# Score matmuls of the recurrence in blocks of 32 instead of 64 columns, in four visits per head instead of two

## The chip, the cores and the metric

The kernel runs on one core of a Trainium2 chip. A core has a matrix engine (TensorE, PE in the profile, with its weight loads listed as PEld), a vector engine (VectorE, DVE), a scalar engine (ScalarE, ACT), GpSimd (POOL) and SyncE (SP), which issues the transfers. The metric is the device time of one execution in microseconds; the kernel before takes 2050.87 us, the median of three runs (2050.38 to 2050.87).

## The reference, cut to what matters

The network has two layers on 1024 tokens of width 1024. Layer 0 is a sliding-window attention, layer 1 a gated linear recurrence (HGRN2); behind each stands a squared-ReLU MLP. The change is in the recurrence, which runs for 8 heads of width 128 over chunks of 64 tokens:

```python
def chunk_step(state, inp):
    qc, kc, vc, lc = inp                       # lc = log of the forget gate
    b = jnp.cumsum(lc, axis=2)
    o_inter = jnp.einsum('bhtd,bhde->bhte', qc * jnp.exp(b), state)
    diff = b[:, :, :, None, :] - b[:, :, None, :, :]
    decay = jnp.exp(jnp.where(causal[None, None, :, :, None], diff, -jnp.inf))
    scores = jnp.einsum('bhtd,bhtsd,bhsd->bhts', qc, decay, kc)
    o_intra = jnp.einsum('bhts,bhse->bhte', scores, vc)
    b_last = b[:, :, -1]
    new_state = jnp.exp(b_last)[..., None] * state + jnp.einsum(
        'bhsd,bhse->bhde', kc * jnp.exp(b_last[:, :, None, :] - b), vc)
    return new_state, o_inter + o_intra
```

The score of token t for an earlier token s in the same chunk is a sum over the 128 features of q at t, k at s, and the product of the forget gates between them, which differs by feature.

## The kernel before, in words

Tiles are 128 partitions by 512 columns (half of the tokens; NH = 2 halves). Large matmuls are done in Strassen form with each float32 operand split into two parts, wh and wl for weights.

The kernel doesn't issue instructions directly. Every operation is recorded (`op`, `mm`, `tt`, `copy`, ...) with an assumed cost; a planner (`Schedule.forward` and `backward`, lines 197 to 356) simulates the engines with these costs four times, and the order that ends first in its own model is issued. So all instructions carry line 433, the line of the common helper, and groups are told apart by tile names: `t`, `a`, `m`, `wr`, `wh`, `wl` are rotating buffers in SBUF, `p` and `q` banks of PSUM (four each), `d` tensors in HBM, `c` constants. A matmul has the form "whole" or "columns" (it uses some of the array's columns only); the planner adds an assumed drain where the form changes.

`recurrence` (line 1513) handles one head. It keeps q and k transposed (features on partitions, 512 tokens in columns). The decay between two tokens is built by doublings: `double` (line 1647) with H = 1, 2, 4, ..., 64 multiplies, in each pair of neighbouring blocks of H tokens, the later block's q and the earlier block's k by the total decay of the other block (VectorE, 256 columns each, four products per doubling and head), and merges the totals. With `apart`, the result goes into a new tile and the unchanged half is copied there by ScalarE (four copies of 256 columns); without, it is done in place. Before, the doublings by 1, 2, 8, 16 and 32 go apart and those by 4 and 64 are in place.

After the doubling by H, the product of k and q is right for pairs of tokens that lie in neighbouring blocks of H tokens: level lg (H = 1 << lg). So the scores of a chunk are assembled from the diagonal (`own`: q and k themselves), six levels, and `cross`, which takes two chunks of 64 together, because everything behind the scores works on 128 tokens. A matmul of a level has one chunk of 64 keys as stationary operand and the 32 later tokens of the same chunk as moving one. Its 64 output rows are the upper or the lower half of the PSUM partitions, so two groups of columns of the array are used in turn. `merge` writes a level into `scores` with a masked copy on VectorE (`copy_predicated`, 128 partitions by 256 columns).

All these matmuls of a head stand in two bursts, called visits here: the first (lines 1551 to 1565) behind the doubling by 2 with the diagonal and levels 0 to 2, the second (1576 to 1587) behind the doubling by 32 with levels 3 to 5 and the cross. Each matmul lists all operands of its visit as inputs (`late`), so that a visit starts only when all of them are there. Then (1590 to 1597) three copies per half lay the scores into a block of 128 by 128 per pair of chunks, and a memset clears the corner.

`hgrn` (line 1792) runs head e's gates (the input projections, nearly all TensorE) beside head e - 1's recurrence, piece by piece; the last head's recurrence runs beside the first matmuls of the output product (`hgrn_out`, line 1720).

Of the kernel before, what the change touches and what calls it, by code (L numbers as in the profile page):

```python
# [22 lines left out]
TH = T // NH  # L23
# [11 lines left out]
BPH = NBLK // NH  # L35
# [102 lines left out]
HALF = {"ACT": 125.0, "DVE": 105.0}  # L138
# [240 lines left out]
class Net:  # L379
# [1011 lines left out]
    def hgrn_constants(self):  # L1391
        bounds = self.const((P, 2 * KT))
        self.dma(bounds, self.io["lb"], 4 * P * 2 * KT)
        l0, l1 = (bounds[:, i * KT : i * KT + KT] for i in range(2))
        top, e0, e1, lb = (self.const((P, KT)) for _ in range(4))
        self.tt("DVE", top, l0, l1, ALU.max, KT)
        for e, l in ((e0, l0), (e1, l1)):
            self.tt("DVE", e, l, top, ALU.subtract, KT)
            self.act(e, e, AF.Exp, KT)
        self.tt("DVE", lb, e0, e1, ALU.add, KT)  # L1400
        self.op("DVE", self.nc.vector.reciprocal, [lb], [lb], 100, lb, lb)
        self.tt("DVE", e0, e0, lb, ALU.mult, KT)
# [7 lines left out]
        si, ti, bits = (self.t(I32, (P, CH)) for _ in range(3))  # L1410
        self.op("Pool", nc.gpsimd.iota, [si], [], 300, si, pattern=[[0, CH]], base=0, channel_multiplier=1)
        self.op("Pool", nc.gpsimd.iota, [ti], [], 300, ti, pattern=[[1, CH]], base=0, channel_multiplier=0)
        self.ts("DVE", si, si, CH - 1, None, ALU.bitwise_and, None, CH)
        self.tt("DVE", bits, si, ti, ALU.bitwise_xor, CH)
        self.diag = self.const((P, CH))
        self.ts("DVE", self.diag, bits, 0, None, ALU.is_equal, None, CH)
        self.level_mask = []
        for lg in range(LEVELS):
            mask, later = self.const((P, CH), I32), self.t(I32, (P, CH))
            self.ts("DVE", mask, bits, lg, None, ALU.logical_shift_right, None, CH)  # L1420
            self.ts("DVE", mask, mask, 1, None, ALU.is_equal, None, CH)
            self.ts("DVE", later, ti, 1 << lg, None, ALU.bitwise_and, None, CH)
            self.ts("DVE", later, later, 0, None, ALU.is_gt, None, CH)
            self.tt("DVE", mask, mask, later, ALU.mult, CH)
            self.level_mask.append(mask)

    def put_by(self, views):
# [85 lines left out]
    def recurrence(self, e, gates, totals, out):  # L1513

        nc = self.nc
        NC = NH * BPH
        chunk = lambda z, j: z[:, j * CH : j * CH + CH]
        scores = self.t(F32, (P, NC, CH))
# [12 lines left out]

        def merge(lg, part):
            H = 1 << lg
            n = CH // (2 * H)
# [3 lines left out]
            self.op("DVE", nc.vector.copy_predicated, [target], [mask, part], 70 + TH // 2 * 1.04, target, mask, part)  # L1538

        def part_of(bank, i):  # L1540
            return bank[:, i * TH // 2 : (i + 1) * TH // 2].rearrange("p (c t) -> p c t", c=NC)
# [9 lines left out]
        own, low, two = (self.psum("q") for _ in range(3))  # L1551
        own = own.rearrange("p (c t) -> p c t", c=NC)
        late = qs + ks + first + q1 + k1 + q2 + k2
        for hf, (q, k) in enumerate(zip(qs, ks)):
            for c in range(BPH):
                for b in range(2):
                    rows, j = slice(b * CH, b * CH + CH), 2 * c + b
                    self.mm(own[rows, hf * BPH + c], chunk(k, j), chunk(q, j), True, True, CH, 2.06, "columns", late)
        level(0, part_of(low, 0), first, ks, late)
        level(1, part_of(low, 1), q1, k1, late)  # L1560
        level(2, part_of(two, 0), q2, k2, late)
        self.tt("DVE", scores, own, self.diag.unsqueeze(1).to_broadcast([P, NC, CH]), ALU.mult)
        merge(0, part_of(low, 0))
        merge(1, part_of(low, 1))
        merge(2, part_of(two, 0))
        qs, ks = q2, k2
        yield
        at, tot, qs, ks = self.double(4, qs, ks, tot, tots, at)
# [7 lines left out]
        low, top, cross = (self.psum("q") for _ in range(3))  # L1576
        late = qs + ks + q4 + k4 + q5 + k5 + q6 + k6
        level(3, part_of(low, 0), qs, ks, late)
        level(4, part_of(low, 1), q4, k4, late)
        level(5, part_of(top, 0), q5, k5, late)  # L1580
        cross = cross[:CH].rearrange("p (c t) -> p c t", c=NC)
        for hf, (q, k) in enumerate(zip(q6, k6)):
            for c in range(BPH):
                self.mm(cross[:, hf * BPH + c], chunk(k, 2 * c), chunk(q, 2 * c + 1), True, True, CH, 3.9, "columns", late)
        merge(3, part_of(low, 0))
        merge(4, part_of(low, 1))
        merge(5, part_of(top, 0))
        qs, ks = q6, k6
        yield
        weights = []  # L1590
        for hf in range(NH):
            s, c = self.t(F32, (P, BPH, 2, CH)), slice(hf * BPH, hf * BPH + BPH)
            self.memset(s[CH:, :, 0].only(0), 0.0, "Pool")
# [9 lines left out]
        for hf, (q, k) in enumerate(zip(qs, ks)):  # L1603
            v, g = back[2 * hf : 2 * hf + 2]
            s = weights[hf]
# [7 lines left out]
            up = self.psum("q").rearrange("p (c e) -> p c e", c=BPH)  # L1613
# [317 lines left out]
```

## Time and profile before

| | |
|---|---|
| Median of 3 runs | 2050.87 us (2050.38 to 2050.87) |
| Profiled execution, first to last instruction (span) | 2048.9 us |
| TensorE busy | 2037.5 us (99%) |
| VectorE busy | 1854.9 us (91%) |
| ScalarE busy | 1306.6 us (64%) |
| GpSimd busy | 57.3 us (3%) |
| Stretch of the eight recurrences | about 950 to 1370 us |

The profile gives the profiled execution's own time as its span, from the first to the last instruction; the runs' times, which also hold what lies around that, are about 2 us longer. A busy TensorE is not TensorE at its peak: matmuls overlap, and the ends of their records are modelled, so the distance between starts says more than the duration of one. A group line reads: line, engine, operation, output<-inputs, shape, count | busy us, mean ns of one | idle time of the engine just before, and what ended it. A float32 matmul leaves more than one record, a matmul of split operands one each.

### The profile page before, as it was taken

How to read it: one execution, taken by the hardware profiler on the slowest of the kernel's cores; microseconds unless marked ns; L12 is line 12 of the kernel's file. 1: busy time of each engine (PE TensorE's matmuls, PEld its weight loads, DVE VectorE, ACT ScalarE, POOL GpSimd, SP SyncE). 2: the span in 40 equal slices, each digit the busy share in tenths (PEclk: the TensorE clock that was granted, in tenths of full speed). 3: DMA queues.
4: the chain of work that ended last, by engine and by line, in shares of the span. 5: the costliest groups of instructions: out<-in, count | busy, mean ns of one | idle time of the engine just before them, and what ended most of it. 6: DMA issues, size and time to landing. Idle time of an engine off the chain costs nothing.

```text
span 2048.9 us, 36889 instructions
## 1 busy us (share of the span) xinstructions
PE 2037.5 (99%) x12300; PEld 1740.4 (85%) x12300; DVE 1854.9 (91%) x3751; ACT 1306.6 (64%) x2711; POOL 57.3 (3%) x120
## 2 busy tenths in 40 slices
PE   9999999999999999999999999999999999999998
PEld 8878888899998888888888888888889999888887
DVE  8899979899999979889988889999999899997985
ACT  7577976667675544657665556666767677544573
POOL 4030000000000000000000000000000000000000
PEclk9999999999999999999999999999999999999999
DMA  6212378788789977665777788988798788997712
GB/s 227 78 52 73 134 262 270 234 273 287 262 291 312 319 264 255 214 205 198 267 267 267 264 272 286 322 287 301 246 297 293 271 286 285 323 323 238 267 52 83
DMA packets 275407, 497.19 MB, mean 243 GB/s; under 512 B 30992, under 2 KB 36368, under 8 KB 275216
## 3 DMA queue, kind: packets, MB, share of 16 engines
q1 hardware_dynamic: 275072, 494.81, 71.6%
q8 instruction: 97, 1.59, 0.3%
q14 instruction: 94, 0.77, 0.1%
q10 hardware_dynamic: 144, 0.02, 0.0%
HBM read 394.57 MB, written 100.14 MB: 241 GB/s over the span
## 4 chain that ended last, share of the span: by engine, by line
PE 93%; DVE 4%; DMA 1%; issue 1%; ACT 0%; SPq 0%; DVEq 0%
PE p L433 50%; PE q L433 44%; DVE t L433 1%; DVE a L433 1%; DVE wl L433 1%; DMA a<-in_wg 1%; DMA a<-in_x 0%; DVE m L433 0%; DVE sm L433 0%; SPq L433 0%; DMA c<-in_sinks 0%; ACT m L433 0%; ACT a L433 0%; DVE c L433 0%; ACT t L433 0%
## 5 line engine op out<-in xcount | busy, mean ns | idle before, releaser
L433 PE MATMUL p<-a,wh 128*128 128x512 f32 (+1 forms) x2832 | 779.4, 360 | 0.3 <-DVE a L433 0.2
L433 PE MATMUL q<-a,wh 128*128 128x512 f32 x2020 | 625.5, 390 | 0.0
L433 PEld LDWEIGHTS p<-a,wh 128*128 128x128 f32 x2832 | 503.0, 189 | 79.6 <-DVE a L433 1.3
L433 PE MATMUL p<-a,wl 128*128 128x512 f32 (+1 forms) x1416 | 503.5, 358 | 0.4 <-DVE wl L433 0.4
L433 PEld LDWEIGHTS q<-a,wh 128*128 128x128 f32 x2020 | 374.9, 188 | 73.8 <-ACT a L433 0.2
L433 PE MATMUL q<-a,wl 128*128 128x512 f32 x1008 | 392.1, 389 | 0.0
L433 ACT CAST wh<-m 128x512 fp32r<-128x512 f32 (+1 forms) x354 | 213.4, 607 | 195.8 <-PE q L433 100.0
L433 ACT CAST wh<-wr 128x512 fp32r<-128x512 f32 (+1 forms) x324 | 194.9, 604 | 172.5 <-PE p L433 104.6
L433 PEld LDWEIGHTS p<-a,wl 128*128 128x128 f32 x1416 | 266.0, 189 | 38.4 <-DVE wl L433 1.1
L433 DVE TENSOR_TENSOR wl<-m,wh 128x512 fp32r<-128x512 f32 (+1 forms) x354 | 234.4, 668 | 37.5 <-ACT wh L433 31.6
L433 DVE TENSOR_TENSOR a<-t,a 128x512 fp32r<-128x512 f32 (+2 forms) x321 | 211.2, 674 | 18.8 <-PE q L433 7.8
L433 DVE TENSOR_TENSOR wl<-wr,wh 128x512 fp32r<-128x512 f32 (+1 forms) x324 | 214.3, 665 | 15.3 <-ACT wh L433 13.5
L433 DVE TENSOR_TENSOR t<-t,t 128x512 f32<-128x512 f32 (+3 forms) x376 | 218.5, 601 | 9.5 <-ACT t L433 7.1
L433 PEld LDWEIGHTS q<-a,wl 128*128 128x128 f32 x1008 | 189.3, 188 | 39.2
L433 ACT ACTIVATE t<-t 128x512 f32<-128x512 f32 x288 | 179.5, 631 | 58.7 <-DVE t L433 47.6
L433 ACT CAST a<-t 128x512 fp32r<-128x512 f32 (+1 forms) x241 | 143.2, 607 | 24.2 <-DVE t L433 9.5
L433 DVE TENSOR_TENSOR t<-t,p 128x256 f32<-128x256 f32 x288 | 115.9, 414 | 15.0 <-PE p L433 11.2
L433 PE MATMUL p<-wh,a 128*128 128x512 f32 x384 | 125.9, 397 | 0.3 <-DVE a L433 0.3
L433 DVE TENSOR_TENSOR m<-wr,wr 128x512 f32<-128x512 f32 (+1 forms) x184 | 118.8, 648 | 0.3
L433 ACT COPY t<-q 128x512 f32<-128x512 f32 (+2 forms) x174 | 95.7, 556 | 20.6 <-PE q L433 16.1
L433 DVE TENSOR_TENSOR a<-a,a 128x512 fp32r<-128x512 f32 (+2 forms) x151 | 100.8, 679 | 7.7 <-ACT a L433 3.2
L433 ACT CAST a<-a 128x512 fp32r<-128x512 f32 x136 | 82.7, 619 | 25.8 <-DVE a L433 21.8
(135 smaller groups left out, 2535.9 us busy)
## 6 DMA issues: line engine op xcount, KB each, us to landing
t<-d SPq DMA_DIRECT2D x592, 256.0 KB, 4.6
a<-d SPq DMA_DIRECT2D x318, 256.0 KB, 4.2
d<-t SPq DMA_DIRECT2D x290, 256.0 KB, 3.3
wr<-in_down SPq DMA_DIRECT2D x224, 256.0 KB, 4.2
wr<-in_up SPq DMA_DIRECT2D x172, 256.0 KB, 4.3
wr<-in_win SPq DMA_DIRECT2D x68, 256.0 KB, 4.1
d<-a SPq DMA_DIRECT2D x64, 256.0 KB, 3.3
wr<-in_wqkv SPq DMA_DIRECT2D x48, 256.0 KB, 3.0
```

The source lines that it names most:

```text
L433: fn(*[place(a) for a in args], **{k: place(v) for k, v in kw.items()})
```

## The change

The score matmuls work on blocks of 32 tokens (QB) instead of chunks of 64.

- The diagonal and levels 0 to 4 take blocks of 32 keys as stationary operand and 32 (diagonal) or 16 (levels) tokens as moving one. The outputs of four neighbouring blocks go to the four quarters of the PSUM partitions, so four groups of columns are used in turn. `scores` and the masks have half the columns; a merge writes 128 columns.
- What was level 5 becomes `top`, matmuls of 32 keys by 32 tokens between the two blocks of a chunk, without a merge; `cross` is cut into matmuls of 32 keys by 64 tokens.
- There are four visits: diagonal and level 0 behind the first product; levels 1 and 2 behind the doubling by 2; levels 3 and 4 behind that by 8; top and cross behind that by 32. Each uses one PSUM bank.
- The doublings by 1 and 16 become in-place ones, so that 1, 4, 16 and 64 are in place and 2, 8 and 32 go apart.
- Laying out the weights takes ten small copies per half (four of the diagonal blocks, four of top, two of cross) instead of three, and three memsets instead of one.
- The planner's assumed costs of these matmuls are changed with it: 1.28 (32 columns) and 1.05 (cross) for 2.06 and 3.9.

```diff
-LEVELS = 6
+QB = 32
+LEVELS = 5
...
-        def level(lg, part, qs, ks, late):
-            H = 1 << lg
+        def level(lg, bank, at, qs, ks, late):
+            n = NC * QB // 2
+            part = bank[:, at * n : at * n + n].rearrange("p (c t) -> p c t", c=NC)
             for hf, (q, k) in enumerate(zip(qs, ks)):
-                for c in range(BPH):
-                    for b in range(2):
-                        rows, j = slice(b * CH, b * CH + CH), 2 * c + b
-                        self.mm(part[rows, hf * BPH + c], chunk(k, j), later(chunk(q, j), H), True, True, CH, 2.06, "columns", late)
+                for j in range(4 * BPH):
+                    rows = slice(j % 4 * QB, j % 4 * QB + QB)
+                    self.mm(part[rows, hf * BPH + j // 4], block(k, j), later(block(q, j), 1 << lg), True, True, QB, 1.28, "columns", late)
+            return part
...
+        def visit(operands):
+            return sum((q + k for q, k in operands), []), self.psum("q")
...
-        at, tot, q1, k1 = self.double(1, first, ks, tot, tots, at, self.t)
+        late, bank = visit([(qs, ks), (first, [])])
+        own = bank[:, TH // 2 :].rearrange("p (c t) -> p c t", c=NC)
+        for hf, (q, k) in enumerate(zip(qs, ks)):
+            for j in range(4 * BPH):
+                rows = slice(j % 4 * QB, j % 4 * QB + QB)
+                self.mm(own[rows, hf * BPH + j // 4], block(k, j), block(q, j), True, True, QB, 1.28, "columns", late)
+        part = level(0, bank, 0, first, ks, late)
+        self.tt("DVE", scores, own, self.diag.unsqueeze(1).to_broadcast([P, NC, QB]), ALU.mult, NC * QB)
+        merge(0, part)
+        at, tot, q1, k1 = self.double(1, first, ks, tot, tots, at)
         yield
         at, tot, q2, k2 = self.double(2, q1, k1, tot, tots, at, self.t)
         yield
...
+        late, bank = visit([(q1, k1), (q2, k2)])
+        parts = [level(1, bank, 0, q1, k1, late), level(2, bank, 1, q2, k2, late)]
+        merge(1, parts[0])
+        merge(2, parts[1])
+        at, tot, qs, ks = self.double(4, q2, k2, tot, tots, at)
         yield
         at, tot, q4, k4 = self.double(8, qs, ks, tot, tots, at, self.t)
         yield
-        at, tot, q5, k5 = self.double(16, q4, k4, tot, tots, at, self.a)
+        late, bank = visit([(qs, ks), (q4, k4)])
+        parts = [level(3, bank, 0, qs, ks, late), level(4, bank, 1, q4, k4, late)]
+        merge(3, parts[0])
+        merge(4, parts[1])
+        at, tot, q5, k5 = self.double(16, q4, k4, tot, tots, at)
         yield
         at, tot, q6, k6 = self.double(32, q5, k5, tot, tots, at, self.t)
         yield
...
+        late, bank = visit([(q5, k5), (q6, k6)])
+        top = bank[:, : NC * QB // 2].rearrange("p (c t) -> p c t", t=QB)
+        cross = bank[:, TH // 2 :].rearrange("p (c t) -> p c t", t=CH)
+        for hf, (q, k) in enumerate(zip(q5, k5)):
+            for j in range(2 * BPH):
+                c, r = j // 2, (j % 2 * 2 + j // 2 % 2) * QB
+                self.mm(top[r : r + QB, (hf * BPH + c) // 2], block(k, 2 * j), block(q, 2 * j + 1), True, True, QB, 1.28, "columns", late)
         for hf, (q, k) in enumerate(zip(q6, k6)):
-            for c in range(BPH):
-                self.mm(cross[:, hf * BPH + c], chunk(k, 2 * c), chunk(q, 2 * c + 1), True, True, CH, 3.9, "columns", late)
+            for j in range(2 * BPH):
+                c, r = j // 2, (j // 2 % 2 * 2 + j % 2) * QB
+                self.mm(cross[r : r + QB, (hf * BPH + c) // 2], block(k, 4 * c + j % 2), block(q, 4 * c + 2, 2), True, True, CH, 1.05,
+                        "columns", late)
...
-            self.copy(s[:CH, :, 0].only(1), scores[:CH, c], 4 * CH, more=HALF["ACT"])
-            self.copy(s[CH:, :, 1].only(2), scores[CH:, c], 4 * CH, more=HALF["ACT"])
-            self.copy(s[:CH, :, 1].only(3), cross[:, c], 4 * CH, more=HALF["ACT"])
+            for b in range(2):
+                up, down = (slice(b * CH + i * QB, b * CH + i * QB + QB) for i in range(2))
+                self.memset(s[down, :, b, :QB].only(f"z{b}"), 0.0, "Pool")
+                for i, rows in enumerate((up, down)):
+                    self.copy(s[rows, :, b, i * QB : i * QB + QB].only(f"d{b}{i}"), scores[rows, c], BPH * QB, more=HALF["ACT"])
+                    self.copy(s[up, i::2, b, QB:].only(f"t{b}{i}"), top[rows, pair], BPH * QB // 2, more=HALF["ACT"])
+                self.copy(s[:CH, b::2, 1].only(f"c{b}"), cross[b * CH : b * CH + CH, pair], BPH * CH // 2, more=HALF["ACT"])
```

More of the change, by code (lines that the diff above doesn't have):

```diff
@@ L1409, in hgrn_constants @@
         nc = self.nc
[L1410 to L1416, printed above, removed]
+        si, ti, bits = (self.t(I32, (P, QB)) for _ in range(3))
+        self.op("Pool", nc.gpsimd.iota, [si], [], 300, si, pattern=[[0, QB]], base=0, channel_multiplier=1)
+        self.op("Pool", nc.gpsimd.iota, [ti], [], 300, ti, pattern=[[1, QB]], base=0, channel_multiplier=0)
+        self.ts("DVE", si, si, QB - 1, None, ALU.bitwise_and, None, QB)
+        self.tt("DVE", bits, si, ti, ALU.bitwise_xor, QB)
+        self.diag = self.const((P, QB))
+        self.ts("DVE", self.diag, bits, 0, None, ALU.is_equal, None, QB)
         self.level_mask = []
         for lg in range(LEVELS):
[L1419 to L1424, printed above, removed]
+            mask, later = self.const((P, QB), I32), self.t(I32, (P, QB))
+            self.ts("DVE", mask, bits, lg, None, ALU.logical_shift_right, None, QB)
+            self.ts("DVE", mask, mask, 1, None, ALU.is_equal, None, QB)
+            self.ts("DVE", later, ti, 1 << lg, None, ALU.bitwise_and, None, QB)
+            self.ts("DVE", later, later, 0, None, ALU.is_gt, None, QB)
+            self.tt("DVE", mask, mask, later, ALU.mult, QB)
             self.level_mask.append(mask)
@@ L1516, in recurrence @@
         NC = NH * BPH
[L1517 to L1518 removed]
+        block = lambda z, j, n=1: z[:, j * QB : (j + n) * QB]
+        scores = self.t()[:, : NC * QB].rearrange("p (c t) -> p c t", c=NC)
         tots, tot = [self.t(tag="m") for _ in range(NH)], [g[1] for g in gates]
@@ L1537, in merge @@
             part = part.rearrange("p c (n h) -> p c n h", n=n)
-            self.op("DVE", nc.vector.copy_predicated, [target], [mask, part], 70 + TH // 2 * 1.04, target, mask, part)
-        def part_of(bank, i):
-            return bank[:, i * TH // 2 : (i + 1) * TH // 2].rearrange("p (c t) -> p c t", c=NC)
+            self.op("DVE", nc.vector.copy_predicated, [target], [mask, part], 70 + NC * QB // 2 * 1.04, target, mask, part)
+        def visit(operands):
+            return sum((q + k for q, k in operands), []), self.psum("q")
         first = [self.t() for _ in range(NH)]
@@ L1550, in recurrence @@
         yield
[L1551 to L1554, printed above, removed]
-            for c in range(BPH):
[L1556 to L1568, printed above, removed]
+        late, bank = visit([(q1, k1), (q2, k2)])
[3 more added lines that the diff above has]
+        at, tot, qs, ks = self.double(4, q2, k2, tot, tots, at)
         yield
```

15 lines of the change are left out of this document (3 added, 12 removed).

## The prediction

> **What bounds the kernel now.** I read the page first, then busy time by stretches, then the chain of waits around one head, then TensorE's own order of time inside one visit of the score matmuls.
>
> ```profile
> span 2048.9 us, 36889 instructions
> PE 2037.5 (99%) x12300; PEld 1740.4 (85%) x12300; DVE 1854.9 (91%) x3751; ACT 1306.6 (64%) x2711; POOL 57.3 (3%) x120
> ...
> q8 instruction: 97, 1.59, 0.3%
> ...
> PE 93%; DVE 4%; DMA 1%; issue 1%; ACT 0%; SPq 0%; DVEq 0%
> ```
>
> ```profile
> 950.00:1370.00 420.00, 419.74 (x3725) 359.08 (x3723) 386.74 (x847) 258.78 (x580) 7.74 (x18) 1.00 0.82 283
> ```
>
> The second fence is the stretch in which all eight heads of the recurrence run (columns: length, busy time and instructions of TensorE, its weight loads, VectorE, ScalarE, GpSimd, then the granted clock and DMA). TensorE has work for 419.74 of 420 us at clock 1.00, and the chain of the whole run is 93% TensorE. So a microsecond taken off TensorE's order here is a microsecond off the span, and work on VectorE (33 us idle), ScalarE (161 us idle) and GpSimd counts only where TensorE comes to wait for it. In this stretch TensorE's waits add up to one:
>
> ```profile
> PE q L433 <- DVE t L433: 0.3, 1, 0.3
> ```
>
> **What the two visits of a head cost now.** The chain around head 0, and TensorE in order of time in its second visit:
>
> ```profile
> 961.55 10.00 PE p L433 x44
> 971.56 3.86 PE q L433 x128
> 975.41 16.55 PE p L433 x72
> 991.96 3.88 PE q L433 x112
> ```
>
> ```profile
> 991.89 2.06 PE L433 MATMUL q<-t,t 128*64 128x32 f32 x64
> 993.78 1.10 PE L433 MATMUL q<-a,a 128*64 128x32 f32 x32
> 994.71 1.12 PE L433 MATMUL q<-t,t 128*64 128x64 f32 x16
> 995.77 0.73 PE L433 MATMUL p<-a,wh 128*128 128x512 f32 x2
> ```
>
> A plain record takes 10.00/44 = 0.227 us. The 72 plain ones behind the first visit take 16.55 instead of 16.36, so a visit costs its 3.86 or 3.88 and 0.19 around it: 4.05 and 4.07 us, **8.13 us a head**, 65 us over eight heads. The code issues 16 matmuls of the diagonal and 48 of three levels in visit one, 48 and 8 (cross) in visit two; the trace has 128 and 112 records, so a float32 matmul leaves two records (the diff's "passes"). The 32 records between 993.78 and 994.71 take 0.93 us, **29.1 ns each**. At that rate 128 records are 3.73 us, so 4.05 - 3.73 = **0.32 us of a visit is entering and leaving** it.
>
> Now how the records lie. Counted in short stretches, TensorE alone, tiles named t (x is how many records run in the stretch): the start of visit one, two column groups in turn, then the cross, which writes one group only.
>
> ```profile
> 971.55:971.59 0.04, 0.04 (x2) 1.00 0.93 358
> 971.59:971.60 0.01, 0.01 (x3) 1.00 0.64 206
> 971.60:971.61 0.01, 0.01 (x4) 1.00 1.69 615
> 971.61:971.65 0.04, 0.04 (x4) 1.00 0.41 154
> 971.65:971.66 0.01, 0.01 (x6) 1.00 0.53 205
> ```
>
> ```profile
> 994.70:994.75 0.05, 0.04 (x1) 1.00 0.84 328
> 994.77:994.81 0.04, 0.04 (x2) 1.00 1.11 410
> 994.83:994.86 0.03, 0.03 (x3) 1.00 1.40 546
> 994.89:994.92 0.03, 0.03 (x4) 1.00 0.70 273
> ```
>
> Both are records of 64 stationary by 64 moving columns. With two groups they come two at a time, a pair each 0.058 us; with one group singly, each 0.058 us. So groups work beside each other, and inside a group a record takes about 58 ns. That is the load of its weights, not its moving columns: the levels move 32 columns and the diagonal 64 at the same pace, and with 128 stationary columns it is
>
> ```profile
> 1361.57 1.72 PE L433 MATMUL q<-t,t 128*128 128x128 f32 x14
> 1363.12 0.43 PE L433 MATMUL q<-t,m 128*128 128x128 f32 x2
> ```
>
> (1363.12 - 1361.57)/14 = 111 ns. From 111 and 58 a straight line gives **about 32 ns for 32 columns** (an estimate).
>
> The Trainium skill, "TensorE: Matmul & The Clock Gate", section "LDWEIGHTS (loading the stationary operand)", has a load's time as columns divided by 1.2: 107, 53 and 27 ns. The trace's 111 and 58 lie some 5 ns above it; by the page four records would take 27 in place of 32 ns, and the gain worked out below would be 4 us larger (416 records of a head by 5/4 ns, eight heads).
>
> **The change, part by part.**
>
> *Score matmuls.* Per head 120 matmuls (240 records) go; 32 of the diagonal, 160 of five levels, 16 "top" and 16 cross come: 224 matmuls, 448 records, each with 32 stationary columns and its output in one of four groups in turn. No row shows four groups. Lower bound: four records per 32 ns, 8.0 each. Upper bound: 29.1 ns each, the rate now, no gain from narrowness. I take a value near the lower end, because the rows show two groups fully beside each other. But the two of a pair start up to 0.01 us apart (x3, then x4, in neighbouring hundredths), and four such starts in a row use up the 32 ns, so I add one of them: 42 per four, **10.5 ns a record** for the 416 that move 16 or 32 columns. The 32 cross records move 64 columns as now, 58 + 10 = 68 per four, 17 each. Body: 416 x 10.5 + 32 x 17 = 4.37 + 0.54 = 4.91 us a head.
>
> *Visits.* Four instead of two: 4 x 0.32 = 1.28 us a head (bounds: 0.19 each, only what lies outside the body, and 0.35).
>
> Together 6.19 against 8.13: **-1.94 us a head, -15.5 us in all.** With the lower bound, 8.0 and 58/4 = 14.6 ns: 3.80 + 1.28 = 5.08, -24.4 us. The change breaks even at (8.13 - 1.28)/448 = 15.3 ns a record.
>
> *Merges and the diagonal's product (VectorE), copies (ScalarE), memsets (GpSimd).*
>
> ```profile
> L433 DVE COPY_PREDICATED t<-c,q 128x256 f32<-128x256 int32 x48 | 25.7, 535 | 3.3 <-PE q L433 1.9
> L433 DVE TENSOR_TENSOR t<-t,t 128x256 f32<-128x256 f32 x32 | 13.1, 418 | 0.8 <-PE q L433 0.6 <-ACT t L433 0.2
> L433 DVE TENSOR_TENSOR t<-q,c 128x512 f32<-128x512 f32 x8 | 5.4, 680 | 0.0
> L433 DVE TENSOR_TENSOR m<-m 128x128 f32<-128x128 f32 x16 | 4.3, 283 | 0.0
> ```
>
> ```profile
> L433 ACT COPY t<-t 128x256 f32<-128x256 f32 x96 | 37.1, 439 | 22.7 <-DVE t L433 17.0 <-PE q L433 5.7
> L433 ACT COPY t<-t 64x256 f32<-64x256 f32 x32 | 12.9, 405 | 17.5 <-DVE t L433 17.2
> L433 ACT COPY a<-t 128x256 f32<-128x256 f32 x32 | 12.1, 403 | 2.0 <-DVE t L433 2.0
> L433 ACT COPY t<-q 64x256 f32<-64x256 f32 x16 | 5.4, 366 | 0.2
> L433 ACT COPY m<-q 128x128 f32<-128x128 f32 x8 | 2.1, 264 | 6.3 <-PE q L433 6.3
> ```
>
> ```profile
> L433 POOL MEMSET t<- 64x256 f32 x16 | 4.7, 306 | 459.5 <-PE q L433 188.1 <-ACT wh L433 138.7 <-DMA a<-d 105.1
> ```
>
> Merges: 48 of 256 columns become 40 of 128, between 283 and 400 ns; with the product (680 to 418) VectorE loses 12 to 16 us. ScalarE loses 64 copies of the doublings by 1 and 16 (32 x 439 + 32 x 403 = 27 us) and the 48 copies into the weights (19 us), and gains 160 small ones at 264 (42 us; bounds 200 and 405, so -14 to +19 net). GpSimd gains 32 memsets of 0.3 us. All of it lies beside TensorE's 420 us and I cost it at nothing; if VectorE were the bound its saving would be worth 12 to 16 us, and if ScalarE's 161 idle us were gone the worst case would cost 19.
>
> *In-place doublings.* Now the doubling by 4 overwrites operands of visit one and the one by 64 those of visit two; after it the doublings by 1, 4, 16 and 64 each wait until their visit has read. Behind such a wait on VectorE stand the next head's weight differences (wl) and the sums before them, for which TensorE would wait. The visits are shorter (about 1.5 for 3.9 us), so each wait can be shorter too. Lower bound nothing; upper bound 16 more waits of 0.3 us, the one that the stage has: 5 us. The last head has no next head under it, but the output product's matmuls stand between its visits, and its last six or so small copies replace three of 0.4 us. I take **+1 us** for both together, nearer to nothing, since TensorE waits 0.3 us in the stage now.
>
> *Sum.* -15.5 + 1 = -14.5: span 2034.4. The runs' median, 2050.87, is 2.0 above the profiled span, so **2036 us**.
>
> **The rivals.**
>
> *Every record costs a fixed time (slower).* No row has a steady mean under 29.1 ns a record. If that is a cost per record whatever its width, 448 records are 13.0 us, with visits 14.3: +6.2 a head, +50, **2100 us**. For it: the matmul count nearly doubles and each does a quarter of the columns. Against it: two groups start within 0.01 us, and the single group's 58 ns is far above the pair's 29, so the time belongs to the group. It decides from 15.3 ns a record. Chance 0.12.
>
> A rule of the Trainium skill speaks for it: the same page, section "Wait — 56ns, not 53.3ns?", has starts never closer than about 25 ns however few columns move, and "TensorEngine Tiling (Array Packing)", section "Instruction Overhead", warns of tiling a dimension that is already small. By 25 ns: 11.2 + 1.28 a head, +35 us, 2086. The pairs above do not obey it as a floor over all groups.
>
> *Two groups at a time.* A matmul's two records share a group; if the order lets only two groups overlap, it is 32 ns per pair: 416 x 16 + 32 x 29.1 = 7.6, with visits 8.9: +0.74 a head, **2056 to 2058**. For it: nothing wider than pairs is shown. Chance 0.08.
>
> *Instruction supply.* q8 brings 97 packets for 12300 TensorE records, 127 each; 0.3% of 16 engines' span is about 1.0 us a packet. A packet lasts 3.7 us in a visit now, 1.3 us after. If the next one is late by half a microsecond in each of 32 visits, 16 us go: **2052**. Against it: visits of 128 records are no longer than one packet, and none stalls now. Chance 0.08.
>
> *New waits* at the four visits or in the last head take half the gain: **2044**. Chance 0.08. The forecast keeps 0.64.
>
> **How the numbers follow.** This kernel's measurement tells about 0.2% (4 us) from no change. Faster: the forecast and most of the last rival, 0.68. Same: instruction supply, rests of the others, 0.10. Slower: fixed cost, two groups, and what supply could cost beyond the gain, 0.22. The likeliest case's own range is 2026 (8.0 ns) to 2044. For 8 in 10 I reach up to two groups at a time, 2057; left out are the fixed cost and a little below.
>
> **What would show it.** Right: records of 32 stationary columns at 8 to 12 ns each, four visits of 1.2 to 1.7 us (the last near 0.8), TensorE's records up by 1664, its busy time in the stage down by some 15 us, VectorE busy down 12 to 16. Wrong: a visit of 128 records over 2.3 us, gaps within a visit, or new TensorE waits for VectorE in the stage of over 4 us.

## The result, and the profile after

| | before | after |
|---|---|---|
| Median of the runs | 2050.87 us (4 runs, 2050.38 to 2051.28) | 2038.97 us (4 runs, 2038.77 to 2040.35) |
| Ratio after/before | | 0.9943 (0.9929 to 0.9957) |
| Span of the profiled execution | 2048.9 us | 2037.1 us |

The forecast was 2036 us (2026 to 2057): the change makes the kernel faster by 11.9 us, 0.58%. One execution among all those below (of the kernel with pauses, 4080.75 us, twice the others) is left out of its median. The page of the changed kernel (engine totals, the queue of instructions with its packets and MB, the shares of the chain of waits):

```profile
span 2037.1 us, 40217 instructions
PE 2019.9 (99%) x13964; PEld 1714.6 (84%) x13964; DVE 1839.6 (90%) x3738; ACT 1310.3 (64%) x2759; POOL 64.9 (3%) x152
...
q8 instruction: 110, 1.80, 0.4%
...
PE 95%; DVE 3%; ACT 1%; issue 1%; DMA 0%; SPq 0%; DVEq 0%; ACTq 0%
```

TensorE has 1664 records more, as reckoned, and still carries the chain. The stretch of the eight recurrences (columns as before), and TensorE's waits in it (us, times, longest):

```profile
950.00:1370.00 420.00, 414.41 (x5451) 344.56 (x5450) 382.94 (x865) 269.46 (x643) 14.96 (x50) 1.00 0.85 290
```

```profile
PE q L434 <- issue: 2.6, 3, 1.6
PE p L434 <- issue: 2.5, 1, 2.5
PE q L434 <- ACT t L434: 0.3, 1, 0.3
```

TensorE is no longer busy without a break: 5.6 us of the 420 are idle, and 5.1 of these are "issue", time in which it waits for nothing that the profile names. No wait for VectorE has come in.

One head after the change, in the chain of waits (start, length, what, count of records), around head 2:

```profile
1068.68 1.26 PE q L434 x85
1069.95 5.66 PE p L434 x24
1075.61 1.32 PE q L434 x110
1076.93 5.66 PE p L434 x24
1082.60 1.30 PE q L434 x109
1083.89 8.38 PE p L434 x36
1092.28 0.88 PE q L434 x63
1093.15 5.67 PE p L434 x24
```

Read as before: 24 plain records at 0.227 us are 5.45, the chain has 5.66, so 0.21 us lie around a visit; the four visits cost 1.47, 1.53, 1.51 and 1.09 us, **5.60 us a head** where the forecast had 6.19 and the kernel before 8.13. Their order of time shows the records and their pace (start, length, count; the last of a row runs 0.18 us on in the records):

```profile
966.24 1.28 PE L434 MATMUL q<-t,t 128*32 128x32 f32 x128
973.13 1.34 PE L434 MATMUL q<-t,t 128*32 128x16 f32 x128
...
990.07 0.95 PE L434 MATMUL q<-t,t 128*32 128x32 f32 x64
```

(1.28 - 0.18)/127 = 8.7 and (1.34 - 0.18)/127 = 9.1 ns a record; I call it **9.0 ns**. Half of the first visit moves 32 columns and the second visit only 16, at nearly one pace.

That is a gain of 8 x 2.53 = 20.2 us in the visits, and only 11.8 us arrive in the span. Here is what takes the rest, in TensorE's order of time, two of its rows with the idle time ahead in brackets:

```profile
1176.41 1.30 PE L434 MATMUL q<-t,t 128*32 128x16 f32 x125
1179.35 0.24 PE L434 MATMUL q<-t,t 128*32 128x16 f32 x3 [1.65 <-issue]
...
1334.59 0.40 PE L434 MATMUL p<-a,wl 128*128 128x512 f32 x1
1337.53 0.63 PE L434 MATMUL p<-a,wh 128*128 128x512 f32 x2 [2.54 <-issue]
```

TensorE stops inside a visit with three records to go, and once between two plain matmuls. From start to start these are 1.83 and 2.94 us; three more stops of 0.62, 0.66 and 0.21 lie in heads 1 and 7, together **6.3 us**. This counts from start to start; 0.3 us of it are the ordinary distances. Counted from the first TensorE record, they stand ahead of numbers 6028, 8059, 9964, 10091 and 10218: neighbours are 127 apart, or multiples of it within one (8059 - 6028 = 16 x 127 - 1). The instruction queue brings 110 packets for 13964 records, 127 each. The rows of that queue in the DMA view (packets, MB, share of 16 engines), for 1171.0 to 1176.9 us and for 1176.9 to 1177.9:

```profile
q8 instruction: 1, 0.02, 1.2%
...
q8 instruction: 1, 0.02, 5.6%
```

One packet lands inside the second microsecond (5.6% of 16 engines is 0.9 us), while TensorE already stands at 1177.5; it goes on at 1179.35, 1.45 us behind the end of that stretch. The stop at 1334.6 looks alike: its packet runs from 1334.86 to 1336.02 and TensorE resumes at 1337.53. The other side of the account is small: two late starts of 0.47 and 0.31 us outside the visits, some 1.4 us of tenths, 0.3 us ahead of the last visit, 0.5 us behind the stage. Most of the tenths, and the late start of the last visit, fall into 3.4 us behind the longest stop, in which the granted clock (third number from the end) was 0.50:

```profile
1338.70:1342.10 3.40, 3.40 (x51) 2.36 (x53) 0.00 (x0) 0.00 (x0) 0.00 (x0) 0.50 0.90 313
```

Compared with the distances of the same records at full clock, they cost about 1.3 us (an estimate). -20.2 + 6.3 + 0.8 + 1.4 + 0.3 + 0.5 = -10.9, against the span's -11.8; some 0.9 us stay open.

Two groups of VectorE (count | busy us, mean ns | idle ahead):

```profile
L434 DVE COPY_PREDICATED t<-c,q 128x128 f32<-128x128 int32 x40 | 14.0, 350 | 0.3
L434 DVE TENSOR_TENSOR t<-q,c 128x256 f32<-128x256 f32 x8 | 3.4, 419 | 0.0
```

Against 25.7 and 5.4 before that is 13.7 us less; the page has VectorE down by 15.3 in all, ScalarE up by 3.7, GpSimd up by 7.6.

### The profile page after: what moved, and what is told of

Its sections match the earlier page's. It is cut to its first block, busy times and chain, and to the rows that moved or that the text cites. A ratio compares the mean times of both kernels' runs of the same rounds, so it can differ in the third digit from the quotient of the medians.

```text
span 2037.1 us, 40217 instructions
## 1 busy us (share of the span) xinstructions
PE 2019.9 (99%) x13964; PEld 1714.6 (84%) x13964; DVE 1839.6 (90%) x3738; ACT 1310.3 (64%) x2759; POOL 64.9 (3%) x152
## 4 chain that ended last, share of the span: by engine, by line
PE 95%; DVE 3%; ACT 1%; issue 1%; DMA 0%; SPq 0%; DVEq 0%; ACTq 0%
PE p L434 52%; PE q L434 43%; DVE t L434 1%; DVE a L434 1%; DVE m L434 0%; DVE wl L434 0%; ACT t L434 0%; DVE sm L434 0%; DMA wr<-in_wqkv 0%; DMA t<-in_x 0%; ACT wh L434 0%; ACT m L434 0%; SPq L434 0%; ACT a L434 0%; DVEq L1912 0%
## 5 line engine op out<-in xcount | busy, mean ns | idle before, releaser
L434 ACT COPY t<-q 128x512 f32<-128x512 f32 (+2 forms) x254 | 111.7, 442 | 30.2 <-PE q L434 24.3
L434 DVE TENSOR_TENSOR t<-t,p 128x256 f32<-128x256 f32 x288 | 116.1, 416 | 15.5 <-PE p L434 11.2
```

Source lines behind the costliest of these rows:

```text
L434: fn(*[place(a) for a in args], **{k: place(v) for k, v in kw.items()})
```

## The experiments

Two things wanted an explanation: why a record takes 9.0 ns, and what the stops are. Except where said, the edits are to the changed kernel and leave nothing out of the computation. The kernel before took 2050.5 to 2050.7 us in these jobs.

### Is the narrow shape needed? The visits alone

The 64-column matmuls of the kernel before, in four visits, with the same in-place doublings (diff against the kernel before):

```diff
-        at, tot, q1, k1 = self.double(1, first, ks, tot, tots, at, self.t)
...
-        late = qs + ks + first + q1 + k1 + q2 + k2
+        late = qs + ks + first
...
         level(0, part_of(low, 0), first, ks, late)
...
+        at, tot, q1, k1 = self.double(1, first, ks, tot, tots, at)
```

> The matmuls of the kernel before (64 columns, two groups, six levels and cross, same merges and copies), but in the changed kernel's four visits and with its in-place doublings (1, 4, 16, 64). Theory that the gain is all in the narrow records: two more visits a head at 0.32 us, 16 x 0.32 = +5 us, and TensorE hides the rest: 2055 to 2057 us, slower than before. Rival, that finer visits or fewer copies on ScalarE (64 less, 27 us) or the shorter stay in PSUM bring part of the gain: 2051 us or less.

Measured: 2056.18 us, ratio 1.0027 (1.0017 to 1.0037). Its chain, one visit and the plain records behind it:

```profile
1081.30 1.99 PE q L433 x64
1083.29 5.66 PE p L433 x24
```

A visit costs 1.99 + 0.21 = 2.20 us, of which 64 records at 29.1 ns are 1.86: the 0.32 to 0.34 us of entering and leaving that the forecast used. Two more visits in eight heads are 16 x 0.32 = 5.1 us, and the kernel is 5.6 us slower. TensorE is busy for 420.00 of 420 us, so the in-place doublings cost it no wait. All of the gain, and more, comes with the narrow shape.

### What sets 9.0 ns? Two groups and one

The matmuls of a visit are issued in another order. In one kernel two column groups alternate for eight matmuls, then the other two; in the other four matmuls in a row (eight records) use one group, then four use the next. (The last visit has half as many in a row.) The work is the same. No run keeps to one group for a whole visit.

```diff
-                for j in range(4 * BPH):
+                for j in sorted(range(4 * BPH), key=lambda j: j % 4 // 2):   # one_group: j % 4
```

> The changed kernel with the matmuls of each visit sorted, so that only two groups of columns take turns at a time (groups 0 and 1 first, then 2 and 3); count and shapes stay. Theory of groups that work beside each other, each held up by the load of its own 32 columns (about 32 ns a record, an estimate): two records per 32 ns, 16 ns a record, so a visit of 128 records has a body of about 2.05 us instead of the 1.15 us of the changed kernel, the last visit 1.4 instead of 0.73: +3.4 us a head, +27 us, less up to 5 us of waits inside visits that the slower pace takes away: 2061 to 2066 us. Rival, a fixed cost of 9 ns per record whatever its group: no change, 2039 us.

> The same, but sorted by single groups: all matmuls of group 0, then 1, 2, 3. Theory of groups beside each other: about 32 ns a record (the cross, 64 moving columns, 58): body of a visit of 128 records 4.1 us, of the last visit 1.0 + 1.9 = 2.9 us: 3 x 2.95 + 2.2 = +11 us a head, +88 us, 2122 to 2127 us. This measures the load of 32 columns, which no row showed. Rival, fixed cost per record: 2039 us.

Measured: 2043.73 us with two groups, 2063.03 with one (one run of each). The same two visits of head 0 in the order of time, two groups and then one:

```profile
965.36 1.58 PE L434 MATMUL q<-t,t 128*32 128x32 f32 x128
972.53 1.64 PE L434 MATMUL q<-t,t 128*32 128x16 f32 x128
```

```profile
965.42 2.73 PE L434 MATMUL q<-t,t 128*32 128x32 f32 x128
973.74 2.73 PE L434 MATMUL q<-t,t 128*32 128x16 f32 x128
```

By (length - 0.18)/127 the mean is 20.1 ns a record in the second order, 11.0 to 11.5 in the first, 9.0 in the changed kernel. Neither expected time came. The pace depends on the order, so it is no fixed cost of a record. But these means mix records of one group with changes from group to group. The start of a visit shows a group by itself. First the order of one group, where the first eight records are all of group 0, then the changed kernel; x is how many records run in the stretch, and none ends yet:

```profile
973.76:973.80 0.04, 0.04 (x2) 1.00 1.37 512
973.81:973.83 0.02, 0.02 (x3) 1.00 1.57 614
973.84:973.86 0.02, 0.02 (x4) 1.00 1.05 410
973.87:973.89 0.02, 0.02 (x5) 1.00 0.79 307
```

```profile
973.13:973.16 0.03, 0.03 (x4) 1.00 1.09 410
973.18:973.21 0.03, 0.03 (x8) 1.00 1.26 478
973.21:973.24 0.03, 0.03 (x12) 1.00 1.07 410
973.24:973.27 0.03, 0.03 (x16) 1.00 1.44 546
```

In one group a new record comes every 0.03 us; the starts in the trace are 52 ns apart once and then 32, 32 and 31. In the changed kernel four come in the same time: 6 or 7 ns from group to group, and from a group's record to its next again 52 ns once and then 32. So a record holds its group for 32 ns, as the forecast's straight line had it, whether it moves 16 or 32 columns; four groups work fully beside each other, and such a stretch goes at **8.0 ns** a record. The mean of 9.0 holds besides it the first step of 52 ns, a step of 45 ns between two levels, and long stretches of 17 ns for two.

Why is the mean of the second order 20 ns and not 32? From the sixth record on its records come in pairs 5 or 6 ns apart, with steps of 25 to 32 ns between: it looks as if the next group began before the last one was through. The trace doesn't name the group of a record, so this is a reading and not shown.

### Are the stops the supply of instructions?

First more records without a break. The narrow matmuls go in two visits of 256 and 192 records, where the visits of before stood, with that kernel's doublings:

```diff
-        late, bank = visit([(qs, ks), (first, [])])
+        late, bank = visit([(qs, ks), (first, []), (q1, k1), (q2, k2)])
+        second = self.psum("q")
...
-        late, bank = visit([(q5, k5), (q6, k6)])
+        late, bank = visit([(qs, ks), (q4, k4), (q5, k5), (q6, k6)])
```

> The narrow matmuls of the changed kernel in the two visits of the kernel before (behind the doublings by 2 and 32), with that kernel's doublings (1, 2, 8, 16, 32 apart; 4, 64 in place): visits of 256 and 192 records. Theory that only the narrow shape matters and a visit costs 0.31 us to enter and leave: two visits less a head, -5 us against the changed kernel, 2034 us. Theory of instruction supply: in the changed kernel TensorE stops inside five visits, each time at a record whose number is 58 or 59 beyond a multiple of 127 (one instruction packet), and goes on about 1.5 us after a packet's transfer; the next packet comes some 4.8 to 5.0 us after the last was begun, so a visit that eats a whole packet in 1.2 us must wait. Visits of 256 and 192 records hold a whole packet nearly always: about 14 stops of 1 to 3.7 us, 42 us in all, against 5 us in the changed kernel: 2034 + 37 = about 2071 us.

Measured: 2080.82 us (one run). Its first visit and the stage:

```profile
970.31 1.61 PE L434 MATMUL q<-t,t 128*32 128x32 f32 x158
975.16 1.48 PE L434 MATMUL q<-t,t 128*32 128x16 f32 x98 [3.24 <-issue]
```

```profile
950.00:1370.00 420.00, 387.90 (x4957) 324.04 (x4955) 348.53 (x776) 261.89 (x641) 13.65 (x47) 0.96 0.77 262
```

It would be the cheaper form by the forecast's own sum (two entries less a head), and it is 42 us slower than the change. Twelve stops of 1.0 to 4.9 us from start to start, all at records 57 to 63 past a multiple of 127, add up to some 39 us; 14 stops and 42 us were expected. The rest of the difference from the expected 2071 is the granted clock, 0.96 in this stage, which I hadn't expected. The trace takes the two apart: behind these stops lie eight stretches of 3.4 or 6.8 us at clock 0.50, where the plain records start 0.427 us apart instead of 0.227. One of them, TensorE alone (16 records in 6.2 us):

```profile
1198.00:1204.20 6.20, 6.20 (x16) 0.50 0.01 3
```

Record by record they cost some 16 us (an estimate). Then the sum closes: the change without its stops and its own half clock is 2039.0 - 6.3 - 1.3, less 16 x 0.32 for the entries, plus 39 and 16: 2081 us, where 2080.8 was measured. So a long unbroken burst pays twice, for the stops and for the clock behind them.

Then the place. 32 matmuls that nobody reads (64 records) are put ahead of the recurrences, at 916.5 us. If the stops hang on the packets, they move to other visits but stay at the same place modulo 127; if they hang on a visit's data, they stay in that visit:

```diff
+        ps = self.psum("q")
+        for _ in range(32):
+            self.op("PE", nc.tensor.matmul, [ps], [self.ident], 222.0, ps[:, :1], self.ident, self.ident[:, :1], start=True, stop=True, form="whole")
```

> The changed kernel with 32 idle float32 matmuls (128 stationary columns, one moving column, result unused) ahead of the recurrences: 64 records of about 0.11 us, +7.1 us, and every later instruction stands 64 records further in its packet of 127. Theory of instruction supply: the stops move with the packets. Those at records 6028 and 8059 (0.6 and 1.8 us) go, there is one of 1.4 to 2.0 us near record 7170 and one of nearly 4 us in the last head near record 10599; all stops lie at the same place modulo 127 as before (58 or 59): 7 us of stops in place of 5, about 2047 to 2048 us. Rival, that the stops belong to the visits themselves (operands that come late, banks): they stay at the same visits, record numbers 64 higher, 2046 us.

Measured: 2044.43 us (2042.09 to 2046.06), ratio 0.9968 (0.9957 to 0.998). Two of its stops in the order of time:

```profile
1094.75 0.27 PE L434 MATMUL q<-t,t 128*32 128x16 f32 x9 [0.94 <-issue]
...
1343.41 0.69 PE L434 MATMUL q<-t,t 128*32 128x16 f32 x59 [0.47 <-issue]
```

Stops stand ahead of records 6919, 8950 and 10220, 60 or 61 past a multiple of 127 as the ones before were 58 or 59; heads 1 and 4 have none in the second visit, where the change had its own. So they move with the packets. My rule for which boundary would stop named other heads and 7 us of stops, where there are 3.0: what decides if a packet is late is not settled.

The sum was 2039.0 - 6.3 + 3.0 + 7.1 for the idle matmuls, 2042.8, which is 1.6 less than measured. Here too the clock is part of it. From 919.0 to 932.7 us, over most of the idle matmuls and some plain ones, it was 0.50. The idle records start 0.213 us apart there instead of 0.111, and the same plain matmul that starts 1.1 us earlier than in the changed kernel at 892 us starts 10.4 us later at 947: the idle matmuls cost 11.4 us and not 7.1. With this, and without the change's own half clock (1.3 us), the sum is 2045.8, now 1.4 too much.

Third, pauses. The three visits of 128 records are cut in two of 64, with plain matmuls between, so that a packet lasts longer:

```diff
-            for hf, (q, k) in enumerate(zip(qs, ks)):
+            for q, k in ((qs[hf], ks[hf]),):
...
         for hf, (q, k) in enumerate(zip(qs, ks)):
+            if hf:
+                yield
...
-            interleave(self.gates(e, streamed if e else x, self.rs, r, got, [None] * 2 if e else begun), before, 14, 12)
+            interleave(self.gates(e, streamed if e else x, self.rs, r, got, [None] * 2 if e else begun), before, 14, 15)
```

> The changed kernel with each of the three visits of 128 records cut in two of 64 (one per half of the tokens), with plain matmuls between: seven visits a head instead of four. Theory: a visit costs 0.31 us to enter and leave, 23 more of them (two pairs stay together) +7 us; no stop inside the visits of heads 0 to 6, since no packet is eaten in one visit; in the last head two stops of together 2.5 us remain, so 5 us of stops become 2.5 to 3: about 2043 us. If stops cost nothing to begin with or stay: 2046 us. If the price of a visit is less when it is short: nearer to 2036 us.

Measured: 2040.30 us (2040.23 to 2040.40), ratio 0.995 (0.993 to 0.997).

```profile
1336.22 1.20 PE L434 MATMUL q<-t,t 128*32 128x16 f32 x108 [1.11 <-issue]
1341.95 0.86 PE L434 MATMUL q<-t,t 128*32 128x32 f32 x56 [1.56 <-issue]
```

No stop is left in the visits of heads 0 to 6. Two stay in the last head, where the plain matmuls are few and visits follow closely (1.29 and 1.76 us from start to start). The trace has 53 bursts where the change has 32: 21 more entries of 0.32 us are 6.7 us. Less 3.2 us of stops and the change's 1.3 us at half clock (this trace has none in the stage) this would be 2.2 slower than the change; measured are 1.3, and nothing is gained either way.

The packet times in the traces tie the stops to their packets: in all 22 stops of these four kernels TensorE goes on 1.2 to 1.6 us behind the landing of a packet of the instruction queue. With one group at a time, where 127 records last 2.5 us, TensorE has no wait at all in the stage. So the stops belong to the packets of the instruction queue and come where records go faster than packets. They keep their place in the packet only roughly: 58 or 59 past a multiple of 127 in the change, 57 to 63 in the other kernels, 69 with the pauses.

### Can a visit be saved?

A visit is 0.32 us plus its records. The diagonal and level 0 can share a matmul: for odd tokens, k divided by the gate (1/gate - 1) makes one stationary operand serve both, so 64 records a head and one visit go. It needs a reciprocal; first by GpSimd's power:

```diff
-        late, bank = visit([(qs, ks), (first, [])])
+            self.tt("Pool", odd, pairs(f)[:, :, 1], self.minus.to_broadcast([P, TH // 2]), ALU.pow, TH // 2)
+            self.ts("Pool", odd, odd, -1.0, None, ALU.add, None, TH // 2)
...
+        late, bank = visit([(qs, ks_near), (q1, k1)])
```

> The changed kernel with the diagonal and level 0 in one set of matmuls: odd tokens' q times their gate as before, even ones' q as it is, and for odd keys k divided by the gate, which with k = 1 - gate is 1/gate - 1 (a power of -1 and a subtraction on GpSimd, idle in the stage). One matmul of 32 by 32 then holds both, 64 records a head fall away, and the remaining 384 stand in three visits of 128: diagonal with levels 0 and 1, levels 2 and 3, level 4 with top and cross. Theory (9 ns a record, 0.31 us a visit, stops by packets): -64 x 9 ns - 0.31 us = -0.89 us a head, -7 us, and stops of 3 to 3.6 us in place of 5: about 2030 us. Rival: GpSimd's power or the in-place scalings come late and TensorE waits for them, or stops in visits grow because all visits are now as long as a packet: 2036 us or more.

Measured: 2648.77 us, ratio 1.2918 (1.2896 to 1.2939).

```profile
L434 POOL TENSOR_TENSOR t<-t,c 128x256 f32<-128x256 f32 x16 | 669.0, 41813 | 218.1 <-DVE t L434 162.2 <-issue 25.2 <-PE p L434 18.0
```

```profile
PE q L434 <- POOL t L434: 601.5, 16, 77.1
```

Power takes 41.8 us each, two a head, and TensorE waits for nearly all of it. The miss is the price of this one operation, which no trace of the case had shown. Then with VectorE's reciprocal:

```diff
-            self.tt("Pool", odd, pairs(f)[:, :, 1], self.minus.to_broadcast([P, TH // 2]), ALU.pow, TH // 2)
-            self.ts("Pool", odd, odd, -1.0, None, ALU.add, None, TH // 2)
+            self.op("DVE", nc.vector.reciprocal, [odd], [f], 1050, odd, pairs(f)[:, :, 1])
+            self.ts("DVE", odd, odd, -1.0, None, ALU.add, None, TH // 2)
```

> The kernel of three visits, with 1/gate - 1 of the odd keys taken by VectorE's reciprocal and a subtraction (256 columns each, two of each a head) in place of GpSimd's power. Estimate for the reciprocal: its row of 4 columns takes 169 ns, a product's of 4 columns 159, so 2.5 ns more a column than nothing, near 1 us for 256; VectorE gains 2.5 us and loses about 0.6 us a head, +15 us in a stretch in which it idles 37 of 420. Theory (9 ns a record, 0.31 us a visit, stops of about 3 us): 2030 to 2033 us, faster than the changed kernel by 6 us or more. Rival: the reciprocal costs 2 us or more, VectorE becomes the bound in the stretch and TensorE waits for it: 2037 us or more.

Measured: 2041.77 us, ratio 0.9962 (0.9948 to 0.9976), not better than the change.

```profile
L434 DVE RECIPROCAL t<-t 128x256 f32<-128x256 f32 x16 | 27.7, 1741 | 0.1
```

```profile
950.00:1370.00 420.00, 411.03 (x4939) 338.19 (x4938) 401.26 (x881) 272.36 (x656) 15.26 (x50) 1.00 0.84 286
```

```profile
PE q L434 <- ACT t L434: 4.1, 8, 0.8
...
PE p L434 <- DVE t L434: 2.2, 2, 1.2
```

The visits came down by 7 us, but a reciprocal takes 1.74 us, 28 in all, and VectorE is now busy for 401 of 420 us. The gain seems to have come back as TensorE's waits for VectorE, and for copies of ScalarE that stand behind it. So I gave the planner the true price, moved the subtraction to GpSimd and the gate's scaling to ScalarE, and ran beside it the changed kernel with that last move alone:

```diff
-            self.op("DVE", nc.vector.reciprocal, [odd], [f], 1050, odd, pairs(f)[:, :, 1])
-            self.ts("DVE", odd, odd, -1.0, None, ALU.add, None, TH // 2)
+            self.op("DVE", nc.vector.reciprocal, [odd], [f], 1741, odd, pairs(f)[:, :, 1])
+            self.ts("Pool", odd, odd, -1.0, None, ALU.add, None, TH // 2)
...
-            self.ts("DVE", f, f, self.f_mul[:, e : e + 1], self.f_add[:, e : e + 1], ALU.mult, ALU.add)
+            self.act(f, f, AF.Identity, bias=self.f_add[:, e : e + 1], scale=self.f_mul[:, e : e + 1])
```

> The kernel of three visits with VectorE's reciprocal, entered into the planner with its measured 1741 ns; the subtraction of 1 goes to GpSimd (0.88 us, measured), and the scaling of the gate (0.57 us on VectorE, 16 times) to ScalarE. VectorE in the stretch falls from 401 to about 388 us. The visits took 41.0 us with the reciprocal and 48.0 in the changed kernel, so the 7 us are there. Theory: they were given back in waits for VectorE and for what waits for it; with 13 us less on VectorE most of them go: 2033 to 2036 us, faster than the changed kernel. Rival: the longer chain in front of the first visit (reciprocal, subtraction, two products) is what TensorE waits for, whatever VectorE's load: 2039 us or more.

> The changed kernel with nothing but the scaling of the gate moved from VectorE to ScalarE: VectorE 9 us less, ScalarE 12 more in the stretch, TensorE's records the same. Theory: TensorE hides VectorE in the changed kernel (its waits for VectorE and ScalarE in the stretch are under 2 us), so no change within 2 us, 2037 to 2041 us, apart from the stops, which move with the order. Rival: VectorE's 383 of 420 us already hold TensorE up: 2035 us or less.

Measured: 2035.68 us (2034.92 to 2038.04), ratio 0.9929 (0.9914 to 0.9944), for three visits with the relief; 2042.8 us (2039.99 to 2044.35), ratio 0.996 (0.9946 to 0.9974), for the changed kernel with the gate's scaling on ScalarE. The stage of each, three visits first:

```profile
950.00:1370.00 420.00, 414.39 (x4965) 343.64 (x4964) 398.15 (x859) 285.66 (x674) 30.61 (x66) 1.00 0.86 290
```

```profile
950.00:1370.00 420.00, 411.62 (x5439) 341.99 (x5438) 375.66 (x844) 281.53 (x657) 14.36 (x50) 1.00 0.84 289
```

With the relief TensorE idles for 5.6 us of the stage instead of 9.0, and the kernel is the fastest here, 3.3 us below the change by the medians. But the intervals of the ratios overlap, and chance can make as much: in the profiled executions (2038.04 and 2038.88 us) its stops at packets add up to 4.2 us from start to start, where the change has 6.3 and 1.3 more at half clock. So it isn't shown that three visits are better. VectorE came down to 398 us only, where 388 was expected, so the cause of the shorter waits is open too. The scaling alone takes 7.3 us off VectorE and gains nothing: the change doesn't wait for VectorE. At 2042.8 us it lies above the expected 2037 to 2041, with more "issue":

```profile
PE q L434 <- issue: 7.5, 4, 2.9
```

Its order of instructions differs a little and other visits meet a packet's end. Its five stops add up to 9.7 us from start to start, 3.4 more than the change's; between the two profiled executions (2040.86 and 2038.88 us) lie 2.0. A kernel that eats packets this fast is sensitive to any edit ahead of it.

## Why the prediction came out as it did

*What bounds the kernel, and what is worth time.* Right. TensorE held the chain (95%), and changes of VectorE by -15.3, ScalarE by +3.7 and GpSimd by +7.6 us were hidden, within the bounds given (-12 to -16, -14 to +19, 32 memsets).

*The price of a visit, 0.32 us.* Right: 1.47 us less 128 records at 9.0 ns is 0.32, and the 64-column visits give the same.

*The pace, 10.5 ns.* This is the term that was mis-sized. It had 32 ns for a load of 32 columns, divided among four groups, and 10 ns more for the starts between them. The first half was right: a group takes a record every 32 ns, and four groups bring four in that time, so the lower bound of 8.0 is the pace of a good stretch. The 10 ns were wrong: the starts of the four groups, 6 or 7 ns apart, lie within the 32. What keeps the mean at 9.0 is the beginning of each burst, the change of level and the slower pairs, none of which the forecast had. The cross took less, too: if the 32 records of top in the last visit go at 9.0 ns (0.29 us) and the last record of cross runs 0.22 us on, the cross ones take (0.95 - 0.22 - 0.29)/32 = 14 ns, against 17. Together 0.59 us a head: -20.2 where -15.5 was forecast.

The Trainium skill, "TensorE: Matmul & The Clock Gate", section "LDWEIGHTS (loading the stationary operand)", gives 27 ns for this load by columns over 1.2. The 32 ns within one group lie 5 ns above it, as the forecast found it for 64 and 128 columns; so far the trace agrees.

*In-place doublings and the last head, +1 us.* The doublings cost nothing that shows: no TensorE wait for VectorE in the stage, and the run with 64 columns in four visits has none either. The late start of the last visit, 0.3 us, fell into the stretch at half clock, so nothing is left for the last head's part.

*Instruction supply, a rival with 0.08.* This is what the forecast lacked. It was priced as half a microsecond in each of 32 visits, 16 us; in fact TensorE stops at five packets, for 0.2 to 2.9 us from start to start, 6.3 us in all. The forecast had named gaps within a visit, and a visit over 2.3 us, as signs that it is wrong; both came, the second visit at 1176.4 us with 3.2. The argument against it failed: that a visit is no longer than one packet doesn't help, because what counts is how fast the visit empties it. The same row that I used, 3.7 us for a packet before and 1.3 after, was the one to believe. That the forecast was only 3 us low is in part luck: this loss and the pace's surplus nearly cancel. -15.5 became -20.2, and +6.3 came in its place, with some 2 us of small waits and half clock.

*A fixed cost per record, 0.12, and two groups at a time, 0.08.* Neither came. 9.0 ns lies below the 15.3 at which the change breaks even, and four groups are quicker than two.

The Trainium skill, the same page, section "Wait — 56ns, not 53.3ns?", has starts no closer than about 25 ns. The traces agree within one group, where the first starts are 31 to 52 ns apart, and not over four: 6 or 7 ns from group to group, 9.0 in the mean.

*New waits, 0.08.* None for data beyond half a microsecond. They did come in the kernel with the reciprocal, where VectorE had only 19 us left.

## What to carry to other kernels

Splitting matmuls that leave columns of the array empty pays as long as groups overlap, and here it came close to what the division among the groups said. To measure the pace of one group, look at the starts within it: a mean over an order that changes groups every few matmuls is another number. When an edit makes an engine's instructions shorter, divide the packet of instructions by the new pace; long bursts of short matmuls then run dry, and merging them cost 42 us here, cutting them in two 1.3. A microsecond saved on the bounding engine can come back as a wait if the next engine is filled to pay for it.

## What the runs showed of the hardware

- With stationary operands of 32 columns in float32 a record starts every 32 ns within a column group and, in steady stretches, every 8.0 over four groups in turn; the means over visits of 128 records are 9.0 ns with four groups in turn, 11.0 to 11.5 and 20.1 in the two other orders. 16 or 32 moving columns make no clear difference; with 64 the cross takes about 14 over four groups.
- TensorE's instructions come in packets of 127 matmul records, about 1 us of transfer each. A packet that was late let TensorE stand until 1.2 to 1.6 us behind its landing; stops of 0.2 to 4.9 us were seen. What triggers the fetch is open.
- Behind some of these stops the granted clock was 0.50 for 3.4 or 6.8 us (0.96 over the stage with visits of 256 and 192 records), and the plain records started 0.427 us apart instead of 0.227.
- A power on GpSimd takes 41.8 us for 128 by 256 float32 values, a reciprocal on VectorE 1.74 us, where a product of that shape takes 0.42.
